# First up stage of the convolution FFN: P1 + P6 summed in PSUM, and the order of four products, for twenty of the 22 features

## The chip, the core and the metric

The kernel runs on one core of a Trainium2 chip. The metric is the device time of one execution in microseconds (us), median of three runs. The engines are named as in the profile: PE (TensorE) multiplies, DVE (VectorE) and ACT (ScalarE) do elementwise work, POOL (GpSimd) does small copies and issues some DMAs, SP (SyncE) issues the other DMAs.

## What is computed

One layer of an encoder for 2048 prompt rows and 128 sample rows of width 1024: attention, an mLSTM, and a convolution FFN. The part that matters here is the first half of the FFN:

```python
def conv_ffn(h, buf, w_up, w_conv, b_conv, w_down):
    u = h @ w_up                       # 1024 -> 2 * 2816
    ext = concatenate([buf, u], axis=1)
    y = b_conv
    for j in range(3):
        y = y + ext[:, j:j + S] * w_conv[j]
    gate, up = split(y, 2, axis=-1)
    return (gelu(gate) * up) @ w_down, ext[:, S:]
```

## The kernel before

The FFN runs in three blocks of rows (`FBLOCKS`), b = 0, 1, 2. Each block has an up stage and a down stage. The up stage goes over 22 features f (128 columns of the gate and the 128 columns of the up half that belong to them) in the order `ORDERS[b]`: 0, 11, 1, 12, 2, 13 and so on. The stage of b = 0 is the first up stage; the change lies in it alone.

For each feature the stage computes a two by two block product by a scheme of seven products instead of eight (Winograd's form of Strassen's). The 768 rows of the block are two halves of 384; seven sums of the activations stand ready in SBUF as tiles `B`. A product is twelve matmuls of 128x384: four pieces of the inner dimension, and for each piece three matmuls (`mm3`), since each fp32 factor is split into a high part (`wuh`, made by a cast on ACT) and a low part (`wul`, made by a subtraction on DVE); the function `split` issues both. So a feature is 7 x 12 = 84 matmuls. The results lie in PSUM: `a` (tile `ua`), `d_` (tile `ub`), and `e` and `c` (the two halves of tile `uec`). Each of these tiles has two buffers, so that feature number n writes into what feature number n-2 of the order has left.

The four weight sums s1 to s4 of a feature (tiles `ws`, line 1344) are formed on DVE in the first block only; POOL writes them to DRAM (`wsd`) for the later blocks. Group g = 0 of a feature's weights is the four factors of P1, P6, P7, P5, group g = 1 the three of P2, P4, P3. Two of three groups go through tiles `wuh`/`wul` with two buffers, the third through four smaller tiles `wu3`. A cast into such a buffer waits until the matmuls of the group that lay there have read it. The raw weights and sums are quarters of 256 KB in eleven buffers (`quad`); SP loads the next ones as these come free.

The combinations of a feature, as the lines stand before: ACT copies `a` to `x1` (line 1638), DVE adds `d_` to give `x2` (line 1640), DVE adds `e` to give `x3` (line 1642), DVE adds `c` for one half of the up result (`second`, line 1501, tile `uu`); ACT copies `a` after P2 was added to it (line 1661, tile `ug`); DVE adds `x2` and `e` after P4 (line 1663), and `x2` and `c` after P3 (line 1501, tile `ug`). The last of these is what frees `uec` for the next feature but one. In the trace x1, x2, x3 are all called `x` (in the order of instructions x0, x1, x2). Then come the convolution (`conv`: ACT line 1520, DVE lines 1521 and 1522, GELU on ACT line 1524), the product of gate and up (line 1673), and the sums of activations for the down stage (`store_a`).

The order of the instructions on each engine is not the order of the code: a scheduler places them by a simulated time line, so a change in one place reorders its neighbourhood on all engines. Each engine then works its own list strictly in order.

Of the kernel before, what the change touches and what calls it, by code (L numbers as in the profile page):

```python
# [13 lines left out]
ALU = mybir.AluOpType  # L14
# [27 lines left out]
FOLD_RATE = 1.0  # L42
FAST = (0, 1, 2)
ORDERS = [[f for k in range(NK) for f in (k, k + NK)] if b in FAST else list(range(NF)) for b in range(3)]
B11, B12, B22, B21 = range(4)
T1, T3, T2, T4 = range(4, 8)
PAIRS += [[(((12, 0), (15, 0)), 0, P, "12"), (((13, 0), (SAMPLE, 0)), P, P, "13"), (((14, 0), (14, 64)), 2 * P, 64, "14")]]
# [3 lines left out]
def hymba_step(ctx: ExitStack, tc: tile.TileContext, I: dict, O: dict):  # L51
    nc = tc.nc
# [50 lines left out]
    def mm3(out, ah, al, bh, bl, start, stop, onto=False):  # L103

        nc.tensor.matmul(out, ah, bh, start=start, stop=False, skip_group_check=onto)  # L105
        nc.tensor.matmul(out, ah, bl, start=False, stop=False, skip_group_check=onto)  # L106
        nc.tensor.matmul(out, al, bh, start=False, stop=stop, skip_group_check=onto)  # L107
# [944 lines left out]
    P1, P6, P7, P5, P2, P4, P3 = range(7)  # L1052
# [13 lines left out]
    def quad(name):  # L1066
        return ffn.p3.tile([P, 512], F32, tag="q", name=name, bufs=11)
# [195 lines left out]
    for n_, (half, gi) in enumerate(seq):  # L1263
# [5 lines left out]
        g = GROUPS[gi]  # L1269
        i = int(g[2])  # L1270
# [61 lines left out]
    def load_quads(b, f, g):  # L1332

        src = lambda i: I["w_up"][f][:, i * 512:(i + 1) * 512]
        if b == 0 and g == 0:
            q = []
            for i in range(4):
                q.append(quad(f"wu{f}_{i}"))
                nc.sync.dma_start(q[i], src(i))
            a11, a12, a22, a21 = q  # L1340
            s1, s2, s3, s4 = [quad(f"ws{f}_{i}") for i in range(4)]
            for o, x, y, op in ((s1, a21, a22, ALU.add), (s2, s1, a11, ALU.subtract), (s3, a11, a21, ALU.subtract),
                                (s4, a12, s2, ALU.subtract)):
                nc.vector.tensor_tensor(o, x, y, op=op)
            for i, o in enumerate((s2, s3, s1, s4)):
                nc.gpsimd.dma_start(wsd[f][:, i * 512:(i + 1) * 512], o)
            raws[f] = [a12, a22, s4]
            return [a11, s2, s3, s1]
        if b == 0:
            return raws.pop(f)  # L1350
        kept = lambda i: wsd[f][:, i * 512:(i + 1) * 512]
        out = []
        for i, s_ in enumerate([[src(0), kept(0), kept(1), kept(2)], [src(1), src(2), kept(3)]][g]):
            r = quad(f"wu{b}_{f}_{g}_{i}")
            nc.sync.dma_start(r, s_)
            out.append(r)
        return out

    def load_up(b, i, g, quads=None):
        f = ORDERS[b][i]  # L1360
        n = 2 * i + g
        nm = f"{b}_{f}_{g}"
        if n % 3 < 2:
            h = wpool.tile([P, 2112], F32R, tag="wh", name=f"wuh{nm}", bufs=2)
            l = wpool.tile([P, 2112], F32R, tag="wl", name=f"wul{nm}", bufs=2)
            at = [(h[:, i * 512:(i + 1) * 512], l[:, i * 512:(i + 1) * 512]) for i in range(4)]
        else:
            t = [p4.tile([P, 1056], F32R, tag="w3", name=f"wu3{nm}_{i}", bufs=4) for i in range(4)]
            at = [tuple(t[2 * x + i // 2][:, i % 2 * 512:i % 2 * 512 + 512] for x in range(2)) for i in range(4)]
        for (h, l), r in zip(at, quads or load_quads(b, f, g)):  # L1370
            split(h, l, r)
        return at
# [111 lines left out]
    for b, tiles in enumerate(FBLOCKS):  # L1484
# [3 lines left out]
        n = HALF[b]  # L1488
# [4 lines left out]
        def product(i, w, acc, onto=False):  # L1493
            for k in range(4):
                c = slice(k * P, (k + 1) * P)
                mm3(acc[:, :n], w[0][:, c], w[1][:, c], B[i][:, 0, k, :n], B[i][:, 1, k, :n],
                    start=not onto and k == 0, stop=k == 3, onto=onto)
# [29 lines left out]
        def ahead_of(i):  # L1527
            if i < 2 * NF:
                pend.append(load_up(b, i // 2, i % 2))
            elif i == 2 * NF:  # L1530
                pend.append(load_product(b, 0, 0) if fast else load_down(0, 0))

        g, parts = {}, {}
        n2 = nt * P // 2

        def fetch(dh, k, early=False):
            if dh > 1 or k >= NF:
                return
            if early:
                g[dh, k] = [quad(f"gr{b}_{dh}_{k}_{i}")[:, :n2] for i in range(2)]  # L1540
                for i, r in enumerate(g[dh, k]):
                    nc.sync.dma_start(r, gd[b][k][:, i * n2:(i + 1) * n2])
            else:
                g[dh, k] = row(f"gr{b}_{dh}_{k}")
                nc.sync.dma_start(g[dh, k][:, :2 * n2], gd[b][k][:, :2 * n2])
# [17 lines left out]
        def fetch_a(i):  # L1563
            if i >= 6 * len(SEQUENCE):
                return
            p, c = divmod(i, 6)
            src = ad[b, SEQUENCE[p][0]]
            ks = slice(2 * c, min(2 * c + 2, NK))
            n_ = (ks.stop - ks.start) * wide(p)
            if i < 5:  # L1570
                g[i] = [quad(f"ar{b}_{i}_{x}")[:, :384] for x in range(2)]
                for x, r in enumerate(g[i]):
                    nc.sync.dma_start(r, src[:, 2 * c + x, :])
            else:
                g[i] = row(f"ar{b}_{i}")[:, :n_]
                nc.sync.dma_start(g[i], src[:, ks, :].rearrange("p k n -> p (k n)"))
# [44 lines left out]
        unfinished = []  # L1621
        for fi, f in enumerate(ORDERS[b]):
            w = pend.pop(0)
            ahead_of(2 * fi + 2)
            if fi >= 3:
                next(done, None)
            if fi == NF - 2:
                for i in range(2):
                    if fast:
                        fetch_a(i)  # L1630
                    else:
                        fetch(0, i, True)
            nm = f"{b}_{f}"
            a, d_, ec = ps_mm(f"ua{nm}"), ps_sm(f"ub{nm}"), ps_big(f"uec{nm}")
            e, c = ec[:, 0:512], ec[:, 512:1024]
            x1, x2, x3 = [p4.tile([P, 384], F32, tag="x", name=f"x{i}_{nm}", bufs=3) for i in range(3)]
            product(P1, w[0], a)
            nc.scalar.copy(x1[:, :n], a[:, :n])
            product(P6, w[1], d_)
            nc.vector.tensor_tensor(x2[:, :n], x1[:, :n], d_[:, :n], op=ALU.add)  # L1640
            product(P7, w[2], e)
            nc.vector.tensor_tensor(x3[:, :n], x2[:, :n], e[:, :n], op=ALU.add)
            product(P5, w[3], c)
            uu = u_tile(f"uu{nm}")
            second(uu, x3, c)
            w = pend.pop(0)
            ahead_of(2 * fi + 3)
            if fi == NF - 1:
                if fast:
                    split_a(0)  # L1650
                    split_a(1)
                    for i in range(2, 5):
                        fetch_a(i)
                else:
                    split_g(0, 0, w3_tile)
                    split_g(0, 1, w3_tile)
                    for k in range(2, 5):
                        fetch(0, k, True)
            ug = u_tile(f"ug{nm}")
            product(P2, w[0], a, onto=True)  # L1660
            nc.scalar.copy(ug[:, 2:2 + n], a[:, :n])
            product(P4, w[1], e, onto=True)
            nc.vector.tensor_tensor(uu[:, 2:2 + n], x2[:, :n], e[:, :n], op=ALU.add)
            product(P3, w[2], c, onto=True)
            second(ug, x2, c)
            yu = conv(uu, 1, f)
            yg = conv(ug, 0, f)
            gt = yg if fast and not last else row(f"g{nm}")
            gv, ov = (lambda t: t[:, :npr]), gt[:, :npr]
            if last:  # L1670
                gv = lambda t: t[:, :npr].rearrange("p (a n) -> p a n", a=2)
                ov = gt[:, :768].rearrange("p (a n) -> p a n", a=2)[:, :, 0:256]
            nc.vector.tensor_tensor(ov, gv(yg), gv(yu), op=ALU.mult)
            if last:
                sv = lambda t: t[:, npr + 2:npr + 2 + DB * (DS + 2)].rearrange("p (b s) -> p b s", b=DB)[:, :, 0:DS]
                nc.vector.tensor_tensor(gt[:, 256:384].rearrange("p (b s) -> p b s", b=DB),
                                        sv(yg), sv(yu), op=ALU.mult)
            if fast:
                store_a(f, gt)
            else:  # L1680
                nc.gpsimd.dma_start(gd[b][f][:, :nt * P], gt[:, :nt * P])
# [5 lines left out]
        if fast:  # L1687
# [73 lines left out]
            kept = {}  # L1761
# [22 lines left out]
            for p, (_, _, set_, onto) in enumerate(SEQUENCE):  # L1784
                for c in range(3):
# [19 lines left out]
                    for k in range(4 * c, min(4 * c + 4, NK)):  # L1805
                        i = 6 * p + k // 2
# [193 lines left out]
```

## Time and profile before

| | |
|---|---|
| median of 3 runs | 2754.65 us (2751.52 to 2759.46) |
| profiled execution | 2753.91 us, its span 2752.2 us |
| PE busy | 97% of the span |
| DVE, ACT, POOL busy | 70%, 53%, 27% |
| first up stage | from 1321 us to about 1648 us of the span |
| of this, 1343 to 1648 us (305 us) | PE busy 301.73, DVE 288.73, ACT 153.86, POOL 167.30 us |

How to read it: the span is the time between the first and the last instruction of the profiled execution. A matmul is shown with its own duration, which overlaps that of the next one; what counts on a full PE is the distance from one start to the next. A bracket behind a row of the time line gives how long the engine stood idle before the instruction, and which engine and line released it.

### The profile page before, as it was taken

How to read it: one execution, taken by the hardware profiler on the slowest of the kernel's cores; microseconds unless marked ns; L12 is line 12 of the kernel's file. 1: busy time of each engine (PE TensorE's matmuls, PEld its weight loads, DVE VectorE, ACT ScalarE, POOL GpSimd, SP SyncE). 2: the span in 40 equal slices, each digit the busy share in tenths (PEclk: the TensorE clock that was granted, in tenths of full speed). 3: DMA queues.
4: the chain of work that ended last, by engine and by line, in shares of the span. 5: the costliest groups of instructions: out<-in, count | busy, mean ns of one | idle time of the engine just before them, and what ended most of it. 6: DMA issues, size and time to landing. Idle time of an engine off the chain costs nothing.

```text
span 2752.2 us, 47852 instructions
## 1 busy us (share of the span) xinstructions
PE 2677.0 (97%) x16323; PEld 2504.0 (91%) x16323; DVE 1922.8 (70%) x3643; ACT 1457.1 (53%) x2961; POOL 731.5 (27%) x1397
## 2 busy tenths in 40 slices
PE   8999999999999999999999999999999999999998
PEld 7899999998899998878999997799999878999976
DVE  5344456646556667766999997758888866998956
ACT  4355545634356666543555456655455665554554
POOL 1000010211100002344465551123343212556401
PEclk9999999999999999999999999999999999999999
DMA  5534355557564456678776668757886867798875
GB/s 185 159 115 141 104 162 169 165 149 213 155 192 131 139 171 223 195 235 279 286 210 197 198 199 286 239 185 209 240 238 184 263 227 233 228 263 233 252 265 178
DMA packets 337172, 557.04 MB, mean 202 GB/s; under 512 B 62083, under 2 KB 168415, under 8 KB 336799
## 3 DMA queue, kind: packets, MB, share of 16 engines
q1 hardware_dynamic: 252846, 400.31, 47.2%
q0 software_dynamic: 45488, 119.84, 14.8%
q10 hardware_dynamic: 38592, 33.83, 3.7%
q8 instruction: 128, 2.10, 0.3%
q14 instruction: 118, 0.96, 0.1%
HBM read 389.77 MB, written 173.49 MB: 205 GB/s over the span
## 4 chain that ended last, share of the span: by engine, by line
PE 43%; DVE 4%; DMA 3%; issue 1%; ACT 1%; POOL 0%; SPq 0%; DVEq 0%; POOLq 0%; ACTq 0%
PE uec L105 5%; PE uec L106 5%; PE uec L107 5%; PE dn L107 3%; PE dn L105 3%; PE dn L106 3%; PE ua L107 3%; PE ua L106 3%; PE ua L105 3%; PE dnm L107 1%; PE dnm L106 1%; PE ub L107 1%; PE dnm L105 1%; PE ub L105 1%; PE ub L106 1%
## 5 line engine op out<-in xcount | busy, mean ns | idle before, releaser
L105 PE MATMUL uec<-B,wuh 128*128 128x384 f32 (+1 forms) x720 | 236.2, 328 | 6.0 <-DVE ug L1501 3.3
L106 PE MATMUL uec<-B,wuh 128*128 128x384 f32 (+1 forms) x720 | 235.3, 327 | 0.0
L107 PE MATMUL uec<-B,wul 128*128 128x384 f32 (+1 forms) x720 | 234.4, 327 | 0.0
L1327 ACT CAST wuh<-wu 128x512 fp32r<-128x512 f32 x255 | 141.7, 618 | 105.9 <-PE uec L106 104.5
L107 PE MATMUL dn<-wdh,al 128*128 128x512 f32 x462 | 186.0, 403 | 4.7 <-DVE al L1328 4.5
L1328 DVE TENSOR_TENSOR al<-ar,ah 128x768 fp32r<-128x768 f32 (+2 forms) x141 | 108.6, 779 | 116.4 <-ACT ah L1327 114.1
L105 PE MATMUL dn<-wdh,ah 128*128 128x512 f32 x462 | 183.8, 398 | 5.9 <-ACT ah L1327 3.7
L106 PE MATMUL dn<-wdl,ah 128*128 128x512 f32 x462 | 182.6, 395 | 0.0
L1327 ACT CAST ah<-ar 128x768 fp32r<-128x768 f32 (+2 forms) x141 | 96.2, 692 | 152.3 <-PE dnm L106 112.9
L1328 DVE TENSOR_TENSOR wul<-wu,wuh 128x512 fp32r<-128x512 f32 x255 | 164.5, 685 | 2.4 <-ACT wuh L1327 2.4
L406 DVE CUSTOM_DVE_ANT_0 tmp<-s,nb 128x640 f32<-128x640 f32 (+4 forms) x128 | 94.4, 738 | 89.9 <-PE s L396 89.3
L105 PE MATMUL vo<-wi_h,hT 128*128 128x256 f32 x544 | 155.2, 285 | 0.6 <-DVE mt L212 0.6
L107 PE MATMUL vo<-wi_h,hT 128*128 128x256 f32 x544 | 155.6, 286 | 0.0
L106 PE MATMUL vo<-wi_l,hT 128*128 128x256 f32 x544 | 154.8, 285 | 0.0
L1328 DVE TENSOR_TENSOR wdl<-wdr,wdh 128x512 fp32r<-128x512 f32 x231 | 145.5, 686 | 8.5 <-ACT wdh L1327 8.3
L105 PEld LDWEIGHTS uec<-B,wuh 128*128 128x128 f32 x720 | 135.2, 188 | 9.2 <-issue 3.7
L106 PEld LDWEIGHTS uec<-B,wuh 128*128 128x128 f32 x720 | 135.4, 188 | 0.2
L107 PEld LDWEIGHTS uec<-B,wul 128*128 128x128 f32 x720 | 135.1, 188 | 0.0
L105 PE MATMUL qk<-hT,wi_h 128*128 128x384 f32 (+1 forms) x384 | 129.0, 336 | 5.9 <-ACT qk_st L237 5.2
L419 DVE TENSOR_TENSOR ptl<-pt,pth 128x640 fp32r<-128x640 f32 (+4 forms) x128 | 93.6, 738 | 57.8 <-ACT pth L418 56.9
L1327 ACT CAST wdh<-wdr 128x512 fp32r<-128x512 f32 x231 | 127.5, 620 | 11.3 <-PE uec L106 7.5
L407 ACT ACTIVATE tmp<-tmp,mn 128x640 f32<-128x640 f32 (+4 forms) x128 | 97.6, 763 | 64.2 <-DVE mn L406 61.8
(426 smaller groups left out, 9258.8 us busy)
## 6 DMA issues: line engine op xcount, KB each, us to landing
wu<-in_w_up SPq DMA_DIRECT2D x220, 256.0 KB, 4.8
wu<-wsd SPq DMA_DIRECT2D x176, 256.0 KB, 3.4
wdr<-wtd SPq DMA_DIRECT2D x132, 256.0 KB, 4.8
wi_raw<-in_w_in SPq DMA_DIRECT2D x52, 512.0 KB, 4.0
wdr<-in_w_down SPq DMA_DIRECT2D x99, 256.0 KB, 4.7
wsd<-ws POOLq DMA_DIRECT2D x88, 256.0 KB, 4.3
ar<-ad_S SPq DMA_DIRECT2D x50, 384.0 KB, 3.4
kraw<-kTd SPq DMA_DIRECT2D x112, 128.0 KB, 3.3
```

The source lines that it names most:

```text
L105: nc.tensor.matmul(out, ah, bh, start=start, stop=False, skip_group_check=onto)
L106: nc.tensor.matmul(out, ah, bl, start=False, stop=False, skip_group_check=onto)
L107: nc.tensor.matmul(out, al, bh, start=False, stop=stop, skip_group_check=onto)
L406: nc.vector.tensor_tensor_reduce(o_, s_, b_, 1.0, 3e38, ALU.add, ALU.min, accum_out=mn)
L407: nc.scalar.activation(tmp[:, :n], tmp[:, :n], AF.Exp, bias=mn, scale=-1.0, accum_out=rsum[:, i % 4, hh:hh + 1])
L419: nc.vector.tensor_tensor(s.ptl[:, sl, qc], ptv, s.pth[:, sl, qc], op=ALU.subtract)
L1327: nc.scalar.copy(h, r)
L1328: nc.vector.tensor_tensor(l, r, h, op=ALU.subtract)
```

## The change

For 20 of the 22 features of the first up stage (the list `SEEDED`: block 0, from the third feature of the order on) `x1 + d_` is no longer an addition on DVE. ACT copies `a`, which holds P1, into the PSUM tile `d_`. P7 is computed next, and then P6 is accumulated by the matmuls onto `d_`. ACT then copies `d_` out to `x2`. The order of the products becomes P1, P7, P6, P5, and the two factors and their sums change places in the lists of weights accordingly; the rest of the feature stays.

```diff
+SEEDED = [(b, f) for b in (0,) for f in ORDERS[b][2:]]
...
-            return [a11, s2, s3, s1]
+            return [a11, s3, s2, s1] if (b, f) in SEEDED else [a11, s2, s3, s1]
...
+        early = (kept(1), kept(0)) if (b, f) in SEEDED else (kept(0), kept(1))
-        for i, s_ in enumerate([[src(0), kept(0), kept(1), kept(2)], [src(1), src(2), kept(3)]][g]):
+        for i, s_ in enumerate([[src(0), *early, kept(2)], [src(1), src(2), kept(3)]][g]):
...
+            seeded = (b, f) in SEEDED
             product(P1, w[0], a)
-            nc.scalar.copy(x1[:, :n], a[:, :n])
-            product(P6, w[1], d_)
-            nc.vector.tensor_tensor(x2[:, :n], x1[:, :n], d_[:, :n], op=ALU.add)
-            product(P7, w[2], e)
+            if seeded:
+                nc.scalar.copy(d_[:, :n], a[:, :n])
+                product(P7, w[1], e)
+                product(P6, w[2], d_, onto=True)
+                nc.scalar.copy(x2[:, :n], d_[:, :n])
+            else:
+                nc.scalar.copy(x1[:, :n], a[:, :n])
+                product(P6, w[1], d_)
+                nc.vector.tensor_tensor(x2[:, :n], x1[:, :n], d_[:, :n], op=ALU.add)
+                product(P7, w[2], e)
             nc.vector.tensor_tensor(x3[:, :n], x2[:, :n], e[:, :n], op=ALU.add)
             product(P5, w[3], c)
```

On each engine the instructions outside the first up stage and the start of the down stage behind it stand in the same order as before. Inside the stage the order is new. Counted in matmuls from the first one of the stage (1848 in all), the products stand as follows at three neighbouring features (first matmul to the one behind the last; a product can be interleaved with others):

| product | f15 before | f15 after | f5 before | f5 after | f16 before | f16 after |
|---|---|---|---|---|---|---|
| P1 | 732-758 | 732-756 | 780-816 | 768-816 | 900-916 | 912-926 |
| P6 | 734-768 | 770-782 | 816-840 | 840-852 | 902-926 | 936-948 |
| P7 | 768-780 | 756-768 | 840-852 | 828-840 | 904-936 | 914-936 |
| P5 | 824-836 | 816-828 | 888-900 | 876-888 | 960-972 | 972-984 |
| P2 | 781-805 | 782-806 | 852-876 | 852-876 | 936-960 | 948-972 |
| P4 | 854-866 | 854-866 | 940-952 | 900-912 | 988-1000 | 1008-1020 |
| P3 | 876-888 | 888-900 | 972-984 | 951-963 | 1043-1055 | 1046-1058 |

The pattern repeats: before, every third feature (252 matmuls) P7 begins 16 matmuls after the last P3 matmul of the feature whose `uec` buffer it takes. The six such places are P7 of f13, f4, f16, f7, f19 and f10. After, the distance at these six is 14, 17, 14, 14, 17 and 14.

VectorE's list around the place where the buffer of `uec` is freed for feature 16. In the names the first number behind the letters is the block, the second the feature, the last a running number; `ws0`, `ws1` of a feature are two of its weight sums (here `ws6_0` is the first sum of feature 6, made of two freshly loaded quarters), `ug0_15` is the addition that frees the buffer. First the list before:

```order
L1663 TENSOR_TENSOR uu0_15_17885<-x1_0_15_17832,uec0_15_17830 128x384
L1673 TENSOR_TENSOR y0_4_0_17788<-y0_4_0_17788,y0_4_1_17782 128x768
L1642 TENSOR_TENSOR x2_0_5_17995<-x1_0_5_17994,uec0_5_17992 128x384
L1344 TENSOR_TENSOR ws6_0_18125<-wu6_3_18123,wu6_2_18121 128x512
L1615 TENSOR_TENSOR s3_0_4_17953<-y0_4_0_17788 128x384
L1521 SCALAR_TENSOR_TENSOR y0_15_1_17937<-uu0_15_17885,wcv_16366,y0_15_1_17937 128x768
L1344 TENSOR_TENSOR ws6_1_18126<-ws6_0_18125,wu6_0_18117 128x512
L1501 TENSOR_TENSOR ug0_15_17895<-x1_0_15_17832,uec0_15_17830 128x384
```

The same stretch after (line numbers of the changed code: 1345 is the old 1344, 1503 the old 1501, 1524 the old 1522, 1672 the old 1663):

```order
L1672 TENSOR_TENSOR uu0_15_17885<-x1_0_15_17832,uec0_15_17830 128x384
L1682 TENSOR_TENSOR y0_4_0_17788<-y0_4_0_17788,y0_4_1_17782 128x768
L1345 TENSOR_TENSOR ws6_0_18125<-wu6_3_18123,wu6_2_18121 128x512
L1617 TENSOR_TENSOR s3_0_4_17953<-y0_4_0_17788 128x384
L1523 SCALAR_TENSOR_TENSOR y0_15_1_17937<-uu0_15_17885,wcv_16366,y0_15_1_17937 128x768
L1345 TENSOR_TENSOR ws6_1_18126<-ws6_0_18125,wu6_0_18117 128x512
L1503 TENSOR_TENSOR uu0_5_18047<-x2_0_5_17995,uec0_5_17992 128x384
L1329 TENSOR_TENSOR wu30_16_1_3_18052<-ws16_3_17973,wu30_16_1_1_18050 128x512
L1524 SCALAR_TENSOR_TENSOR y0_15_1_17937<-uu0_15_17885,wcv_16366,y0_15_1_17937 128x768
L1503 TENSOR_TENSOR ug0_15_17895<-x1_0_15_17832,uec0_15_17830 128x384
```

Between the first weight sum and the addition that frees the buffer stand three more instructions now, and the addition `x2_0_5` stands ahead of this stretch.

PE's list at the first two matmuls of P2 of feature 3, which use the first quarter of group 1 of its weights (`wuh0_3_1`). Before:

```order
L106 MATMUL uec0_3_17358<-B2_0_15356,wuh0_3_0_17162 128x384
L107 MATMUL uec0_3_17358<-B2_0_15356,wul0_3_0_17163 128x384
L105 MATMUL ua0_14_17509<-B0_0_15354,wu30_14_0_0_17324 128x384
L105 MATMUL ua0_3_17356<-B4_0_16344,wuh0_3_1_17251 128x384
L106 MATMUL ua0_3_17356<-B4_0_16344,wuh0_3_1_17251 128x384
```

After (106, 107, 108 are the old 105, 106, 107):

```order
L106 MATMUL uec0_13_17194<-B3_0_16340,wuh0_13_0_17007 128x384
L107 MATMUL uec0_13_17194<-B3_0_16340,wuh0_13_0_17007 128x384
L108 MATMUL uec0_13_17194<-B3_0_16340,wul0_13_0_17008 128x384
L106 MATMUL ua0_3_17356<-B4_0_16344,wuh0_3_1_17251 128x384
L107 MATMUL ua0_3_17356<-B4_0_16344,wuh0_3_1_17251 128x384
L106 MATMUL uec0_13_17194<-B5_0_16348,wu30_13_1_0_17096 128x384
```

P2 of feature 3 now begins directly behind the last matmuls of P5 of feature 13, that is, behind the last readers of `wuh0_13_0`. The same stands at feature 18 behind feature 7.

ACT's list around the copy of P1 at feature 16. Before:

```order
L1520 ACTIVATE y0_15_0_17943<-ug0_15_17895,wcv_16366 128x768
L1661 COPY ug0_5_18059<-ua0_5_17990 128x384
L1638 COPY x0_0_16_18148<-ua0_16_18145 128x384
L1524 ACTIVATE y0_15_0_17943<-y0_15_0_17943 128x768
L1520 ACTIVATE y0_5_1_18101<-uu0_5_18047,wcv_16366 128x768
```

After (1642 is the copy onto `d_`, 1645 the copy out of it, 1522 the old 1520, 1526 the old 1524):

```order
L1670 COPY ug0_5_18059<-ua0_5_17990 128x384
L1522 ACTIVATE y0_15_0_17943<-ug0_15_17895,wcv_16366 128x768
L1642 COPY ub0_16_18146<-ua0_16_18145 128x384
L1522 ACTIVATE y0_5_1_18101<-uu0_5_18047,wcv_16366 128x768
L1645 COPY x1_0_16_18149<-ub0_16_18146 128x384
L1526 ACTIVATE y0_15_0_17943<-y0_15_0_17943 128x768
```

The copy onto `d_` follows an instruction that reads what DVE's `ug0_15` wrote, and a second copy has come in ahead of the GELU.

## The prediction

> **What bounds the kernel now.** I read the page first, then the busy time in the stretch that the change touches.
>
> ```profile
> span 2752.2 us, 47852 instructions
> PE 2677.0 (97%) x16323; PEld 2504.0 (91%) x16323; DVE 1922.8 (70%) x3643; ACT 1457.1 (53%) x2961; POOL 731.5 (27%) x1397
> ...
> 1343.00:1648.00 305.00, 301.73 (x1714) 298.93 (x1713) 288.73 (x451) 153.86 (x245) 167.30 (x252) 0.99 0.66 201
> ```
>
> The second row is the page's busy time by engine, the last one the stretch of the 20 changed features (length, then busy us of PE, weight loads, DVE, ACT, POOL). PE is full there, and DVE is the next: 288.73 of 305 us, 95%. ACT has half its time free. So the change takes work from the second engine, not from the first, and can win only what PE loses by waiting. What that is, the time line of PE tells. The rows show start, duration, and in the bracket the idle time before it with its releaser.
>
> ```profile
> 1394.00 0.44 PE L107 MATMUL ua<-B,wul 128*128 128x384 f32 x1
> ...
> 1481.72 0.33 PE L106 MATMUL ub<-B,wuh 128*128 128x384 f32 x1
> 1483.52 0.41 PE L105 MATMUL uec<-B,wuh 128*128 128x384 f32 x1 [1.47 <-DVE ug L1501]
> ...
> 1484.31 0.34 PE L105 MATMUL ua<-B,wuh 128*128 128x384 f32 x1
> ...
> 1527.49 0.33 PE L106 MATMUL ub<-B,wuh 128*128 128x384 f32 x1
> ...
> 1571.98 0.33 PE L106 MATMUL ub<-B,wuh 128*128 128x384 f32 x1
> 1573.94 0.41 PE L105 MATMUL uec<-B,wuh 128*128 128x384 f32 x1 [1.62 <-DVE ug L1501]
> ...
> 1574.95 0.52 PE L106 MATMUL ua<-B,wuh 128*128 128x384 f32 x1
> ...
> 1578.15 0.38 PE L106 MATMUL ub<-B,wuh 128*128 128x384 f32 x1
> ...
> 1620.03 0.45 PE L107 MATMUL ua<-B,wul 128*128 128x384 f32 x1
> ```
>
> From 1484.31 to 1527.49 lie 248 matmuls: 0.1741 us each is PE's undisturbed step. The rows at 1394.00 and 1620.03 are the same place of the pattern (the first low-part matmul of P1 of f13 and of f10), five periods of 252 matmuls apart: 226.03 us, against 1260 x 0.1741 = 219.4. So PE loses 6.7 us over 15 of the 20 features. It loses it at one kind of place, P7 waiting for the addition `ug` that frees its `uec` buffer: at f16 (1481.72 to 1484.31, four steps) 2.59 - 0.70 = 1.89 us, at f19 (1571.98 to 1574.95, five steps) 2.97 - 0.87 = 2.10, and then at half speed (1574.95 to 1578.15, ten steps in 3.20 us) 1.46. The other three places share 1.2. Part of each is a slow restart: from 1483.52 to 1484.31 three steps take 0.79 us, 0.27 too much. Why DVE is late there, its own time line shows:
>
> ```profile
> 1434.44 0.69 DVE L1344 TENSOR_TENSOR ws<-wu,wu 128x512 f32<-128x512 f32 x1 [1.26 <-DMA wu<-in_w_up]
> ...
> 1480.21 0.69 DVE L1344 TENSOR_TENSOR ws<-wu,wu 128x512 f32<-128x512 f32 x1 [2.79 <-DMA wu<-in_w_up]
> 1480.82 0.55 DVE L1615 TENSOR_TENSOR s<-y 128x384 f32<-128x384 f32 x1
> 1481.29 1.01 DVE L1521 SCALAR_TENSOR_TENSOR y<-uu,wcv,y 128x768 f32<-128x768 f32 x1
> 1482.22 0.68 DVE L1344 TENSOR_TENSOR ws<-ws,wu 128x512 f32<-128x512 f32 x1
> 1482.82 0.55 DVE L1501 TENSOR_TENSOR ug<-x,uec 128x384 f32<-128x384 f32 x1
> ...
> 1524.69 0.69 DVE L1344 TENSOR_TENSOR ws<-wu,wu 128x512 f32<-128x512 f32 x1 [1.50 <-DMA wu<-in_w_up]
> ...
> 1570.64 0.69 DVE L1344 TENSOR_TENSOR ws<-wu,wu 128x512 f32<-128x512 f32 x1 [2.95 <-DMA wu<-in_w_up]
> ```
>
> Once in a period the first weight sum of a feature waits for the loads of its raw weights, and everything behind it in DVE's list is late. Waits of 2.79 and 2.95 us cost PE the two big stops; waits of 1.26 and 1.50 us nearly nothing. About 1.3 us is slack. And the load, by the chain of waits, starts when a split of weights on DVE has freed a raw buffer:
>
> ```profile
> 1562.60 0.70 DVE wul L1328
> 1563.32 7.23 DMA wu<-in_w_up
> ```
>
> **The change part by part.** *The addition removed, the copy added.*
>
> ```profile
> L1640 DVE TENSOR_TENSOR x<-x,ub 128x384 f32<-128x384 f32 x19 | 10.4, 549 | 0.0
> ...
> 1412.04 0.34 PE L107 MATMUL ua<-B,wul 128*128 128x384 f32 x1
> ...
> 1412.41 0.48 ACT L1638 COPY x<-ua 128x384 f32<-128x384 f32 x1 [1.20 <-PE ua L107]
> ```
>
> DVE loses 20 x 0.549 = 11.0 us, and is then busy 277.7 of 305 (91%). ACT gains 20 x 0.48 = 9.6 us on 153.9. Neither is on the path by itself: the sum of both is nothing, as long as ACT's copy is there in time.
>
> *The new wait of P6 for the copy onto `d_`.* The rows at 1412 give it: the copy starts 0.37 us after the last P1 matmul started and takes 0.48. From the end of an addition on DVE to the matmul that waited for it (1482.82 + 0.55 to 1483.52) 0.15 us pass; I take the same from ACT. So P6 may start 1.00 us after P1's last matmul started. By the order 10 matmuls stand between at f3, f4, f16, f18, f19 and f10, at the others 12 to 24: at least 11 x 0.1741 = 1.91 us. P7 hides the copy with 0.91 us to spare, and the cost is 0. No row here shows a copy written to PSUM; the rows bound it by 0.48 into SBUF below and by the 0.91 of spare above (a copy would have to take three times as long to be seen). The Trainium skill (ScalarE: Activation LUTs, "Step-by-step: what each stage is for") says that PSUM is the faster target for ScalarE; that would only add to the spare, and no run here shows it.
>
> *The places where DVE frees `uec`.* At f16, as the lists show, PE now gives 48 matmuls from P4 of f15 to P7 instead of 38: 10 x 0.1741 = 1.74 us more for DVE. DVE has three more instructions between the weight sum and `ug`: by the steps in the rows above (0.47 for 384 elements, 0.60 for 512, 0.93 for the convolution) 2.00 us more. The load comes earlier: the split that frees its buffer waits for P5 of f15, which ends at matmul 828 instead of 836, 1.39 us, less one weight sum that has moved ahead of the split, 0.60. Sum: 1.74 - 2.00 + 0.79 = 0.53 us in favour of the change. I take it for all the places: f16 and f19 gain 0.53 each, the three small ones (0.4 each) vanish, 1.2. The half speed came behind a gap of 1.96 us and not behind one of 1.80 (1481.72 to 1483.52); with the gap at f19 at 1.43 I take it as gone, 1.46. Together -3.7 us. Bounds: 0, if the loads land as late as before, and -6.7, if all goes.
>
> The Trainium skill (TensorE: Matmul & The Clock Gate, "Part 1: The HAM clock gate") has PE fall to half clock after an idle window of about 3.4 us. The trace disagrees with the length of the idle time, 1.96 us here, and the measurement decides; by the page the half speed would not hang on this stop, and the sum would be 1.5 us higher.
>
> *New waits for casts.* P2 of f3, and of f18, now stands directly behind P5 of the feature whose weight buffer it takes.
>
> ```profile
> 1405.24 0.34 PE L106 MATMUL uec<-B,wuh 128*128 128x384 f32 x1
> ...
> 1405.65 0.62 ACT L1327 CAST wuh<-wu 128x512 fp32r<-128x512 f32 x1 [1.74 <-PE uec L106]
> ```
>
> These rows show the same hand-over before: the cast starts 0.41 us after the last reader of the buffer started, takes 0.62, and with 0.15 the first matmul can start 1.18 us behind that reader. The new order gives it two steps, 0.35: a stop of 0.83 and a restart of 0.27, 1.1 us, twice. P1 of f4, and of f19, stands five steps behind the last such reader (0.87): 0.31 + 0.27, 0.6 us, twice. Together +3.4 us. Bounds: 0, if that buffer is freed by another group, and 5.2, if each of the four costs a full 1.3 (no step of cover).
>
> **The sum**, against the profiled execution's 2753.9: -3.7 + 3.4 = -0.3, so 2753.6. The median before is 0.7 above that execution, well within the runs' range; as a median I forecast 2754.3: no change. All shares below count by 0.3%, 8.3 us, about what a measurement of this kernel can tell from no change.
>
> **The rivals.**
>
> *A, the stage runs without a gap.* If DVE's 11 us of relief bring the loads so early that no place stops and the casts are hidden, the whole 6.7 us go: 2747.2, as a median 2748. For it speaks that DVE's share falls from 95 to 91%; against it that three instructions have moved ahead of `ug`. To pass 8.3 us the waits at the start of the down stage must go too, 2.1 us by the rows of PE's waits:
>
> ```profile
> PE dn L105 <- ACT wdh L1327: 1.7, 2, 1.2
> PE dn L105 <- ACT ah L1327: 0.4, 1, 0.4
> ```
>
> that is 2745.1. Chance of A 0.19, of it 0.06 beyond 0.3%.
>
> *B, slower: the copy onto `d_` stands in ACT's queue behind an instruction that waits for DVE, and PE waits with it.* ACT does wait like that:
>
> ```profile
> L1524 ACT ACTIVATE y<-y 128x768 f32<-128x768 f32 x19 | 16.1, 847 | 51.9 <-DVE y L1522 51.9
> ```
>
> 2.7 us each time. If a wait like it stands ahead of the copy at the six places with 1.91 us of cover, each stops PE for 2.7 - 0.91 + 0.27 = 2.1 us: 12.4 in all, 2766.0, as a median 2767. If half speed follows every stop, 1.46 each time, it is 2775. It decides from about 2 us of lateness at all six (1.4 us each make 8.3). Against it: in ACT's new list none of the six copies comes directly behind line 1524; at f16 it follows the convolution's first step, whose input `ug` is due 22 matmuls, 3.8 us, before P6. For it: `ug` has moved back on DVE, and the queue gives nothing back. Chance 0.20.
>
> *C, the loads set the pace, and DVE's relief changes nothing.* The stops stay as they are and the four new waits come on top: 2753.9 + 3.4 = 2757.3, as a median 2758. For it: the wait that counts is one for DMA, of 7.23 us in the row above. Against it: its start hangs on a split that the new order frees earlier. Chance 0.16.
>
> **How the numbers follow.** My forecast has 0.45, and with C and most of A everything within 0.3% has 0.45 + 0.16 + 0.13 = 0.74; faster 0.06; slower 0.20. The range goes from A, 2748, to the lighter form of B, 2767; outside are the rest of A and the heavy form of B, some 0.15.
>
> **What would show it.** Right: in the stretch DVE is busy about 11 us less and ACT 10 us more; PE waits less for `ug` at line 1503, about 2 us for casts at two places before P2 of `ua` and two before P1, and not at all for ACT's copy before `ub`. Wrong: waits of `ub` for line 1642 (B), or the same brackets of 1.5 us behind `ug` (C), or a distance from the first place to the last of 219.4 us (A).

## The result and the profile after

The changed kernel takes 2765.32 us (median of 6 runs, 2760.73 to 2769.30) against 2754.58 (6 runs) for the kernel before. The ratio on record is 1.0032, 95% interval 1.0019 to 1.0046 (the quotient of the two medians is 1.0039). Two repetitions gave 1.0050 (1.0033 to 1.0066) and 1.0027 (1.0013 to 1.0041). So it is slower by about 0.3 to 0.5%, 7 to 14 us. The forecast was no change.

The page of the changed kernel, and the same 305 us of the stage as before (they begin 22 us behind the first matmul of the stage in both):

```profile
span 2766.0 us, 47853 instructions
PE 2682.6 (97%) x16323; PEld 2509.7 (91%) x16323; DVE 1914.6 (69%) x3623; ACT 1465.0 (53%) x2981; POOL 723.5 (26%) x1397
1352.45:1657.45 305.00, 297.25 (x1682) 293.54 (x1682) 276.55 (x424) 160.28 (x262) 164.19 (x249) 0.99 0.66 199
```

DVE is busy 12.2 us less (288.73 to 276.55) and ACT 6.4 us more (153.86 to 160.28). The forecast had 11 and 10 for the whole set of features, and the 305 us now hold a little less of the stage. But PE, the engine that is full, is busy 4.5 us less in the same time and has done 32 matmuls less. The waits of PE in the stage say for what (who waited, for which engine and line; us in total, times, longest). First before, then after:

```profile
PE uec L105 <- DVE ug L1501: 3.3, 3, 1.6
PE ua L107 <- DVE wul L1328: 1.2, 2, 0.7
PE uec L105 <- DVE x L1642: 0.7, 1, 0.7
PE dn L105 <- ACT wdh L1327: 0.5, 1, 0.5
```

```profile
PE uec L106 <- DVE x L1651: 4.3, 3, 1.8
PE uec L106 <- ACT wuh L1328: 2.2, 1, 2.2
PE ua L108 <- DVE wul L1329: 1.3, 2, 0.9
PE ua L106 <- ACT wuh L1328: 1.1, 2, 0.5
PE uec L106 <- DVE uu L1503: 0.7, 2, 0.5
```

The row for `ug` is gone: in this profile P7 no longer waits for it. Instead PE waits 4.3 us for `x` (x3), where it was 0.7 before, and at one place 2.2 us before P4. The first of the three waits for `x` (0.7) lies at the stage's start, as before. The other two are P5 of f14 and of f8. ACT, DVE and PE at f14, from the time line:

```profile
1443.90 0.46 ACT L1645 COPY x<-ub 128x384 f32<-128x384 f32 x1
...
1445.94 0.69 DVE L1345 TENSOR_TENSOR ws<-wu,wu 128x512 f32<-128x512 f32 x1 [1.62 <-DMA wu<-in_w_up]
...
1448.35 0.69 DVE L1345 TENSOR_TENSOR ws<-ws,wu 128x512 f32<-128x512 f32 x1
1448.95 0.55 DVE L1651 TENSOR_TENSOR x<-x,uec 128x384 f32<-128x384 f32 x1
...
1447.45 0.33 PE L107 MATMUL ua<-B,wuh 128*128 128x384 f32 x1
1449.55 0.45 PE L106 MATMUL uec<-B,wu 128*128 128x384 f32 x1 [1.77 <-DVE x L1651]
```

x2 is there at 1444.36. The addition x3, which needs only x2 and P7, starts 4.6 us later, because in DVE's list it stands behind two weight sums of f15, and the first of them waits 1.62 us for its load. In the code P5 writes the half `c` of `uec`, while x3 reads the half `e`; the row shows that P5 waited for it all the same, so the wait is taken for the whole tile. Before, x3 stood one row ahead of those sums at this place:

```profile
1432.63 0.55 DVE L1642 TENSOR_TENSOR x<-x,uec 128x384 f32<-128x384 f32 x1
1434.44 0.69 DVE L1344 TENSOR_TENSOR ws<-wu,wu 128x512 f32<-128x512 f32 x1 [1.26 <-DMA wu<-in_w_up]
```

The new order also left P5 less room: between P6 and P5 of f14, and of f8, lie 26 matmuls, 4.5 us, where before it was 48, 8.4 us. P4 of f5 is the same, with `uu` in place of x3, behind the sums of f6:

```profile
1494.34 0.69 DVE L1345 TENSOR_TENSOR ws<-wu,wu 128x512 f32<-128x512 f32 x1 [3.33 <-DMA wu<-in_w_up]
...
1496.94 0.55 DVE L1503 TENSOR_TENSOR uu<-x,uec 128x384 f32<-128x384 f32 x1
...
1497.64 0.41 PE L106 MATMUL uec<-B,wuh 128*128 128x384 f32 x1 [2.17 <-ACT wuh L1328]
```

The bracket names ACT, one of whose casts ended at the same time as `uu`, 1497.49. It is `uu` that counts: in the second profile of the changed kernel that cast ended only after the same matmul had started, and the row names `uu`:

```profile
1488.70 0.41 PE L106 MATMUL uec<-B,wuh 128*128 128x384 f32 x1 [1.85 <-DVE uu L1503]
```

In DVE's list of waits, the weight sums before and after (same 305 us):

```profile
DVE ws L1344 <- DMA wu<-in_w_up: 10.7, 6, 2.9
...
DVE ws L1345 <- DMA wu<-in_w_up: 14.9, 11, 3.3
```

DVE, with less to do, waits for its loads more often: of the 12.2 us by which it is less busy, 4.2 are these waits (they are 9.6 and 17.6 us in the next profiles of the two kernels).

**Where the time lies.** Every profile has the same 16323 matmul records, so two matmuls mark the same points in all kernels: the first of the stage, and one of the second up stage, 2597 records later. Of before, then after:

```profile
1320.96 0.34 PE L105 MATMUL ub<-B,wuh 128*128 128x384 f32 x1
...
1826.09 0.34 PE L107 MATMUL ua<-B,wul 128*128 128x384 f32 x1
```

```profile
1330.41 0.34 PE L106 MATMUL ub<-B,wuh 128*128 128x384 f32 x1
...
1838.35 0.34 PE L108 MATMUL ua<-B,wul 128*128 128x384 f32 x1
```

505.1 us and 507.9. So of the 13.4 us between the two profiled executions only 2.8 lie in the stage and the down stage behind it (5.6 lost up to the down stage's first matmul, 2.8 given back in the down stage); 9 lie ahead of the stage, where both kernels have the same instructions in the same order. The table holds these stretches for all profiles (us, between the starts of matmuls in the traces; the first column begins at the program's first matmul, the third ends at its last), with the ratio to the kernel before, which was measured anew for each group of runs.

| kernel | to the stage | the stage and its down stage | the rest | ratio (95%) |
|---|---|---|---|---|
| before | 1312.7 | 505.1 | 917.0 | |
| before, again | 1313.9 | 502.4 | 916.4 | 1.0005 (0.9994-1.0015) |
| changed | 1321.8 | 507.9 | 918.6 | 1.0032 (1.0019-1.0046) |
| changed, 2nd | 1314.9 | 508.0 | 918.2 | 1.0050 (1.0033-1.0066) |
| changed, 3rd | 1312.0 | 510.6 | 918.8 | 1.0027 (1.0013-1.0041) |
| order alone | 1318.9 | 499.6 | 914.6 | 0.9997 (0.9987-1.0008) |
| seeding alone | 1312.0 | 505.1 | 920.4 | 1.0007 (0.9997-1.0017) |
| P6 last | 1315.2 | 502.9 | 917.6 | 1.0015 (1.0006-1.0024) |
| addition put back | 1309.7 | 512.4 | 915.5 | 1.0011 (1.0000-1.0022) |
| sums behind x3 | 1321.7 | 503.3 | 917.2 | 0.9992 (0.9981-1.0003) |
| sums behind uu | 1316.6 | 503.0 | 919.1 | 1.0011 (1.0000-1.0022) |
| two places pinned | 1319.8 | 505.1 | 917.6 | 1.0004 (0.9991-1.0017) |
| before, sums behind ug | 1312.0 | 497.5 | 915.6 | 0.9972 (0.9960-0.9985) |
| changed, sums behind ug | 1312.3 | 494.6 | 917.8 | 0.9976 (0.9962-0.9989) |

### The profile page after: what moved, and what is told of

Its sections match the earlier page's. It is cut to its first block, busy times and chain, and to the rows that moved or that the text cites. A ratio compares the mean times of both kernels' runs of the same rounds, so it can differ in the third digit from the quotient of the medians.

```text
span 2766.0 us, 47853 instructions
## 1 busy us (share of the span) xinstructions
PE 2682.6 (97%) x16323; PEld 2509.7 (91%) x16323; DVE 1914.6 (69%) x3623; ACT 1465.0 (53%) x2981; POOL 723.5 (26%) x1397
## 3 DMA queue, kind: packets, MB, share of 16 engines
q0 software_dynamic: 45488, 119.84, 14.9%
## 4 chain that ended last, share of the span: by engine, by line
PE 42%; DMA 4%; DVE 4%; issue 1%; ACT 1%; POOL 0%; DVEq 0%; POOLq 0%; SPq 0%; ACTq 0%
PE uec L106 5%; PE uec L107 5%; PE uec L108 5%; PE dn L108 4%; PE dn L106 3%; PE dn L107 3%; PE ua L108 3%; PE ua L107 2%; PE ua L106 2%; PE dnm L108 1%; PE dnm L107 1%; PE dnm L106 1%; DMA wu<-in_w_up 1%; PE ub L107 1%; PE ub L106 1%
```

## The experiments

**Controls.** Both kernels unchanged, to see which part of the 13.4 us belongs to the change.

> The kernel before, unchanged, as a control. Both theories: ratio 1.000 within 0.1%. The two profiled executions so far differ by 13.4 us at the end, of which 9.2 us were there before the first up stage, where both kernels give the same instructions in the same order. If those 9.2 us are an accident of the execution (T1), this profile's distance from the start to the first matmul of the stage may lie anywhere within some 10 us of the earlier one; if they belong to the changed kernel (T2), it agrees with the first profile of before within 3 us.

> The changed kernel, unchanged, as a control. T1 (the change costs what its own stage shows, about 5 us, and the rest is an accident): ratio 1.001 to 1.0025 and, in its profile, the way up to the stage is no longer than in the control of before by more than 4 us. T2 (something of the change costs outside its stage too): ratio 1.003 to 1.005, and the 9 us ahead of the stage are there again. Both: inside the stage PE stops about 2 us for P5 at f14 and f8 behind x3 on DVE, and about 2.4 us for P4 at f5 behind uu.

The ratio was that of T2 (1.0050), the place was that of T1: the changed kernel came to the stage 1.1 us behind the control of before. The stage with its down stage was 5.6 us longer (508.0 and 502.4), with the same stops and one more behind `uu`, 1.7 us, later in the stage:

```profile
PE uec L106 <- DVE uu L1503: 3.8, 3, 1.8
PE uec L106 <- DVE x L1651: 3.6, 3, 1.6
```

> The changed kernel, unchanged, on the chip of the run with two places pinned, with a third profile. Two questions. The ratio: 1.003 to 1.005 as before. The way up to the stage, where both kernels give the same instructions: 9.2 and 2.1 us longer than in the first profile of before in the two profiles so far. If that is an accident of the half-speed stretches (about 1.7 us each, 1 to 6 of them ahead of the stage in the ten profiles), it goes with their number here too, within 3 us; if it belongs to the changed kernel, it is 4 us or more whatever their number.

The third profile reached the stage 0.7 us earlier than the first of before. The 9 us were an accident of one execution; T2 falls as far as the way up is concerned. The stops were there again (`uu` 4.5 us in all, 2.84 of it at f5; `x` 3.7).

**The two halves of the change apart.** First the new order of products and weights without the seeding:

```diff
             product(P1, w[0], a)
             if seeded:
-                nc.scalar.copy(d_[:, :n], a[:, :n])
+                nc.scalar.copy(x1[:, :n], a[:, :n])
                 product(P7, w[1], e)
-                product(P6, w[2], d_, onto=True)
-                nc.scalar.copy(x2[:, :n], d_[:, :n])
+                product(P6, w[2], d_)
+                nc.vector.tensor_tensor(x2[:, :n], x1[:, :n], d_[:, :n], op=ALU.add)
```

> Products and weights in the new order P1 P7 P6 P5, but P1 is still copied to x1 in SBUF and added to P6 on DVE (no copy onto PSUM, 20 additions of 0.549 us back on DVE, ACT as after). Theory S (the stops come from the order, which puts P5 behind x3, with P6 so late): the stage is as long as in the changed kernel or longer, ratio 1.002 to 1.007, since DVE has 11 us more to do ahead of x3; stops of about 2 us at P5 again. Rival K (the copy onto PSUM on ACT and the matmul that adds onto it are what costs): the stage is as long as before, ratio 0.999 to 1.001.

I had expected the order to be what hurts. Alone it does not: 0.9997, and the stretch is shorter than before (499.6). But this kernel does not set P5 as near behind P6 as the changed kernel does: 48 matmuls lie between them at f14 and 36 at f8, not 26. And x3 of f14 stands ahead of the sums again. No stop of P5 is left but the early one:

```profile
PE ua L106 <- ACT wuh L1328: 1.6, 3, 0.5
PE ua L108 <- DVE wul L1329: 1.0, 2, 0.6
PE uec L106 <- DVE x L1651: 0.7, 1, 0.7
...
DVE ws L1345 <- DMA wu<-in_w_up: 3.1, 3, 1.4
```

With 11 us more to do, DVE waits for loads 3.1 us instead of 14.9. That gave the theory R: the weight sums, and where the scheduler sets them in DVE's list once it has time to spare. The other half, seeding with the old order P1 P6 P7 P5:

```diff
-            return [a11, s3, s2, s1] if (b, f) in SEEDED else [a11, s2, s3, s1]
+            return [a11, s2, s3, s1]
...
-                product(P7, w[1], e)
-                product(P6, w[2], d_, onto=True)
+                product(P6, w[1], d_, onto=True)
                 nc.scalar.copy(x2[:, :n], d_[:, :n])
+                product(P7, w[2], e)
```

> Seeded as in the changed kernel (copy of P1 onto the PSUM tile by ACT, P6 summed onto it, copy out by ACT), but products and weights in the old order P1 P6 P7 P5: the fourth corner beside before, the changed kernel and the one with the new order alone. Theory R (taking the addition off DVE lets the scheduler set the weight sums, which wait for DMA, ahead of the additions x3 and uu that P5 and P4 wait for; the order of the products is innocent): stops at P5 and P4 as in the changed kernel, DVE waits for DMA 10 times or more, ratio 1.002 to 1.005. Rival O (it takes the new order and the seeding together): 0.999 to 1.001.

1.0007: the number is that of O. Half of R held: DVE waits for loads 10 times again.

```profile
DVE ws L1345 <- DMA wu<-in_w_up: 12.4, 10, 2.0
```

But at f14 and f8 x3 stands in its list directly behind the first sum, not four rows behind it, and P5 does not stop there; the two largest stops that are left, 1.4 and 1.5 us start to start, are P7 of f4 and f19. So waiting for loads is not the loss by itself; what counts is what stands behind the wait. Here 34 matmuls lie between P6 and P5 at f14 and f8. Only both halves together set x3 four rows behind the sum and P5 26 matmuls behind P6; this run does not say which of the two makes the stop.

**P6 moved behind P5**, so that P5 no longer comes after x3:

```diff
-            return [a11, s3, s2, s1] if (b, f) in SEEDED else [a11, s2, s3, s1]
+            return [a11, s3, s1, s2] if (b, f) in SEEDED else [a11, s2, s3, s1]
...
                 product(P7, w[1], e)
-                product(P6, w[2], d_, onto=True)
+                product(P5, w[2], c)
+                product(P6, w[3], d_, onto=True)
...
-            product(P5, w[3], c)
+            if not seeded:
+                product(P5, w[3], c)
```

> Seeded as in the changed kernel, but the products come in the order P1 P7 P5 P6: P5 no longer stands behind x3 in any feature, since it is given ahead of the P6 that x3 waits for, and P4 stands 36 matmuls or more behind P5. Theory S: the stops of 2 us at P5 and P4 go, DVE keeps its 11 us of relief, and the stage is 3 to 6 us shorter than in the changed kernel: ratio 0.998 to 1.001. Stops for casts may remain, 1 to 3 us. Rival K (the seeding costs): as long as the changed kernel, 1.002 to 1.005.

1.0015, between the two ranges: the stops of P5 went and the stretch is 5 to 8 us shorter than in the changed kernel, but other waits took part of it back: P4 behind `uu` once, and more at the start for the low part of a weight. That last wait lies ahead of the change; the other profiles have it too, with 0.4 to 1.2 us.

```profile
1326.57 0.44 PE L108 MATMUL ua<-B,wul 128*128 128x384 f32 x1 [1.82 <-DVE wul L1329]
...
1562.50 0.44 PE L106 MATMUL uec<-B,wuh 128*128 128x384 f32 x1 [1.54 <-DVE uu L1503]
```

**The addition put back** as work that nothing uses:

```diff
                 nc.scalar.copy(x2[:, :n], d_[:, :n])
+                nc.vector.tensor_tensor(x1[:, :n], x2[:, :n], d_[:, :n], op=ALU.add)
```

> The changed kernel with 20 additions put back on DVE that nothing uses (x2 + d_ into a tile of x's pool), each where the removed one stood. Everything that the change adds on ACT and PE stays. Theory R: with DVE's time filled again, the weight sums go back behind x3 (no place with two sums ahead of x3, as there are at f14 and f8 in the changed kernel), the two stops of 2.1 us at P5 go, and the kernel gets faster by doing more: 0.999 to 1.0015. Rival A (the copies on ACT, 10 us more and in the chain from P6 to x3, are what costs): no gain, 1.003 to 1.006, or more since DVE has 11 us more to do.

1.0011 is R's number, but it settles little: its interval overlaps that of the changed kernel's third measurement on the same chip, and its profile has the longest stretch of all (512.4). P5 of f14 and f8 do not stop (36 matmuls lie between P6 and P5 there), but a product at the stage's end waits 1.7 us for x3, and the old stops behind `ug` are back, one of them doubled:

```profile
1572.96 0.41 PE L106 MATMUL uec<-B,wuh 128*128 128x384 f32 x1 [3.09 <-DVE ug L1503]
```

**The sums pinned.** In the next kernels nothing is computed otherwise than in the changed kernel; the four sums of a feature are only queued on DVE behind a mark of the feature two places earlier:

```diff
+            i = ORDERS[b].index(f)
+            with tc.issue_after(marks[i - 2]) if i - 2 in marks else nullcontext():
-            for o, x, y, op in (...):
-                nc.vector.tensor_tensor(o, x, y, op=op)
+                for o, x, y, op in (...):
+                    nc.vector.tensor_tensor(o, x, y, op=op)
...
-            nc.vector.tensor_tensor(x3[:, :n], x2[:, :n], e[:, :n], op=ALU.add)
+            x3_ = nc.vector.tensor_tensor(x3[:, :n], x2[:, :n], e[:, :n], op=ALU.add)
+            if seeded:
+                marks[fi] = x3_.ins
```

> The changed kernel, in which the four weight sums of a feature are queued on DVE behind the addition x3 of the feature two places earlier in the order. Theory R: x3 never stands behind a wait for DMA, so the stops at P5 of f14 and f8 (2.15 and 2.10 us, and the half speed behind one of them) go; the one at P4 of f5 (2.5 us) stays, since uu still stands behind a sum there: 2 to 5 us less than the changed kernel, ratio 1.001 to 1.003. Rival A: the stops at P5 stay, since x3 waits for ACT: 1.003 to 1.006.

0.9992, better than R asked: the loss is gone. The stops of P5 went, and P4 of f5 lost 1.01 us (start to start) instead of 2.51. DVE still waits for loads, and the loss is gone all the same:

```profile
DVE ws L1347 <- DMA wu<-in_w_up: 12.3, 10, 2.6
...
PE uec L106 <- DVE uu L1505: 1.4, 3, 0.7
PE ua L108 <- DVE wul L1329: 1.2, 2, 0.8
PE uec L106 <- DVE ug L1505: 0.8, 2, 0.6
```

With the mark at `uu` instead (the addition of `c`):

> The changed kernel, in which the four weight sums of a feature are queued on DVE behind the addition uu (P5's result) of the feature two places earlier in the order, so that neither x3 nor uu stands behind them. Theory R: the stops at P5 and P4 all go, 5 to 7 us less than the changed kernel, ratio 0.999 to 1.002; what could eat that: the sums come later, so casts or low parts of the weights are late (waits of PE for wul or wuh), up to 3 us. Rival A: 1.003 to 1.006.

1.0011, inside R's range. The stops at P5 and P4 are gone and DVE waits for loads only 3.0 us, but the sums come later and PE waits 3.3 us for low parts of weights (four times), as was feared.

Then the mark `if seeded and f in (14, 8)`, so that only the sums of f15 and f9 are pinned:

> The changed kernel, in which only at two places, f14 and f8, the weight sums are queued on DVE behind x3 (sums of f15 and f9); the rest of the order is nearly that of the changed kernel. These are the two places where two sums stood ahead of x3 and PE stopped 2.1 us for P5. Theory R: both stops go, 4 to 6 us with the half speed behind one of them: ratio 1.000 to 1.003, and 4 us or more below the changed kernel on the same chip. Rival D (the loss is spread over many small waits, and the pins of all features together brought it back): at most 1 us less than the changed kernel, 1.003 to 1.005.

1.0004 against 1.0027 for the changed kernel on the same chip: medians of 2753.87 and 2760.32 us, 6.5 us from pins at two places, and rival D falls. At f14 the two rows of DVE have changed places, and P5 has no bracket, although only 24 matmuls lie between P6 and P5 there, two fewer than in the changed kernel. So it is the place of x3 behind the waiting sums that made the stop, not the distance by itself:

```profile
1443.29 0.54 DVE L1653 TENSOR_TENSOR x<-x,uec 128x384 f32<-128x384 f32 x1
1443.75 0.68 DVE L1347 TENSOR_TENSOR ws<-wu,wu 128x512 f32<-128x512 f32 x1
```

Not all of the 6.5 us was lost at the two places themselves. P5 lost 3.3 us there in the third profile of the changed kernel; P4 of f5, whose sums are not pinned, also lost less, 1.31 us from start to start instead of 3.18, and no half speed followed as it did there. Why f5 lost less is not shown.

**The same in the kernel before.** There it was `ug` that stood behind the sums of the feature three places later:

```diff
+            with tc.issue_after(marks[i - 3]) if i - 3 in marks else nullcontext():
...
-            second(ug, x2, c)
+            ug_ = second(ug, x2, c)
+            if b == 0 and fi >= 2:
+                marks[fi] = ug_.ins
```

> The kernel before, in which the weight sums of a feature are queued on DVE behind the addition ug of the feature three places earlier, which frees the PSUM buffer that P7 waits for. No seeding, old order of products. Theory R (what PE loses in this stage is decided by the sums that wait for DMA ahead of what PE waits for): the stops of 1.5 us behind ug go, 2 to 5 us less than before, ratio 0.998 to 0.9995. Rival L (the loads set the pace, and what is gained at ug is lost as late casts or low parts of weights): 0.9995 to 1.001.

0.9972, 2745.19 us: 8 us less than before, and more than theory R asked for. From the stage's first matmul to the one ahead of the down stage's first there are 1823 steps; at 0.1741 us each they take 317.4 us. The kernel before took 9.8 us more (7.1 in its second profile), the changed kernel 15.4 (14.3 and 16.9 in the others), this one 4.3. All that is left of PE's waits in the stage, and no weight sum among DVE's waits any more:

```profile
PE ua L107 <- DVE wul L1328: 1.4, 2, 1.0
PE uec L105 <- DVE x L1643: 0.8, 1, 0.8
PE uec L105 <- DVE uu L1664: 0.5, 2, 0.3
PE dn L105 <- ACT wdh L1327: 0.5, 1, 0.5
```

And the changed kernel with the same pin (`if seeded:` in place of `if b == 0 and fi >= 2:`):

> The changed kernel with the pin that made the kernel before faster: the weight sums of a feature are queued on DVE behind the addition ug of the feature three places earlier. By the order no x3 stands behind a sum then; uu still does at eight features, five to seven rows on. Theory R: the changed kernel loses its stops at P5, the sums come late enough that they seldom wait for DMA (under 5 us in all instead of 15 to 18): ratio 0.997 to 0.9995, and what is left of the change itself, once the order on DVE is mended in both, is 0 to 4 us of loss from casts (four places at 0.5 us) and from P4 behind uu. Rival W (the relief of DVE is worth something once the sums are out of the way): faster than the pinned kernel before, below 0.996.

0.9976, 2743.77 us, and in the trace the shortest stretch of all, 494.6 us (3.8 us above the undisturbed pace in the stage):

```profile
PE ua L108 <- DVE wul L1329: 1.2, 2, 0.7
PE uec L106 <- DVE x L1652: 0.7, 1, 0.7
PE uec L106 <- DVE uu L1505: 0.3, 1, 0.3
```

No wait for a load, and none for a cast at the four places. It is not faster than the pinned kernel before by anything that the intervals show; W falls. With the sums out of the way, no gain and no cost of the change itself can be told from nothing: the medians of the two pinned kernels are 1.4 us apart, and each ratio is known to about 0.13%, 3.6 us.

## Why the prediction was wrong

*What bounds the kernel: right.* PE is full, and what DVE is late with is decided by weight sums that wait for loads. The last two experiments show it: with these sums behind `ug`, 5.5 of the 9.8 us are gone in the stage (2.8 of the 7.1 in the control), and most of what is left lies at its start, ahead of the change.

*"It loses it at one kind of place": the step that failed.* I worked out the new distances for P7 and `ug` alone. But x3 and `uu` read the same tile `uec`, and P5 and P4 write it. Rows of before showed such a wait (P5 of the first feature, 0.7 us for `x` at line 1642), and the order showed that x3 moves from one row ahead of the sums to four rows behind the first of them at f14 and f8. I followed that shift for `ug` only. The order showed besides that P5 comes nearer to P6, from 48 matmuls to 26 at these two features, and I used the new positions for the copy, the casts and P7, not for x3. Its cost: 2.10 and 2.15 us from start to start at P5, 2.51 at P4 of f5, 0.79 and 0.61 at P4 of two more; less a step of 0.174 each that is 7.3, with 1.5 of half speed behind f8 8.8 us. The sum contained 0 for all of it. The kernel pinned at two places shows the cause at P5: with x3 ahead of the sums the two stops are gone, and the kernel is 6.5 us faster, a part of it at f5.

*The places where DVE frees `uec`: right in sign, too small.* -3.7 was forecast; all stops behind `ug` went (1.62, 1.78 and 0.33 us by the same count), and the half speed that followed one of them: -5.2, with the slow restarts nearer to the bound of -6.7. In the other two profiles of the changed kernel a wait of 0.1 and of 0.4 us for `ug` is left. So the advance was larger than the assumed 0.53 us. The stops of PE at P5 and P4 lie ahead of P7 and may have given DVE the time there; no run separates that.

*Casts: right in place, too dear.* 3.4 us forecast, 1.8 measured:

```profile
1424.95 0.34 PE L108 MATMUL uec<-B,wul 128*128 128x384 f32 x1
1425.82 0.45 PE L106 MATMUL ua<-B,wuh 128*128 128x384 f32 x1 [0.53 <-ACT wuh L1328]
...
1446.81 0.34 PE L108 MATMUL ua<-B,wul 128*128 128x384 f32 x1
1447.17 0.44 PE L106 MATMUL ua<-B,wuh 128*128 128x384 f32 x1
```

P2 of f3 loses 0.70 us (1.1 forecast), P1 of f4 0.19 (0.6), and the same at f18 and f19; these losses are counted without the restart, which takes 0.1 us more each time where I had set 0.27. With -5.2, +8.8 and +1.8 the stage comes to +5.4; this pair of traces has +5.6. Other pairs have other sizes: from 9.8 or 7.1 before to 14.3, 15.4 or 16.9 after it is 4.5 to 9.8 us.

*P6's wait for the copy: right.* No row has `ub` waiting for line 1642. The two copies:

```profile
L1645 ACT COPY x<-ub 128x384 f32<-128x384 f32 x20 | 9.5, 475 | 22.1 <-PE ub L108 22.1
L1642 ACT COPY ub<-ua 128x384 f32<-128x384 f32 x20 | 9.3, 463 | 18.2 <-PE ua L108 18.1
```

The Trainium skill's statement that PSUM is ScalarE's faster target (ScalarE: Activation LUTs, "Step-by-step: what each stage is for") agrees in sign: 463 against 475 ns.

*The rivals.* B had nearly the right number, 2767, by a mechanism that did not occur; that was luck. C was right that relief of DVE does not bring loads earlier (waits for them grew from 10.7 to 14.9 us), but wrong that the old stops stay. What came was a third: with time to spare on DVE the scheduler set the sums ahead of what PE waits for next, while P5 moved nearer to P6.

*What stays open.* The ratios put the loss at 7 to 14 us, the medians at 7 to 11. The three traces show 4.5 to 9.8 in the stage, of which 3 to 8 are left at the end of its down stage, and 1 to 2 behind that, where the spread among all kernels (914.6 to 920.4) is larger than that. The rest I could not place: the way up to the stage varies from 1309.7 to 1321.8 us by itself. Not tried: `e` and `c` as tiles of their own, which might take the wait of P5 for x3 away without a pin.

## What to carry to other kernels

When an engine is relieved and a scheduler orders it, look at what moves up into the room: an instruction that waits for DMA, set ahead of one that the full engine waits for, can cost more than the work that was saved is worth. For a tile whose halves are used by different instructions, list every reader and writer at its new distance, not only the one that waits now. And a wait is worth removing only with a view to what is queued behind it: pinning the sums behind one addition took 8 us from the kernel before and brought the changed one to the same time, while the kernel pinned behind x3 ran at 0.9992 with 12 us of DVE's waits for loads still in it.

## What I had not expected of the hardware

In the traces' records of the granted clock every stretch of half speed starts a whole multiple of 3.413 us from the others of its execution and lasts 3.413 us, or twice that (the last one of each runs past the program's end). In the stage and its down stage, over 14 profiles, half speed came eight times. To see what it followed, count in each 3.413-us cell of this grid by how much the starts of matmuls lie further apart than the undisturbed step (0.174 us for 384 columns, 0.232 for 512). Half speed followed the cells with 2.06 to 3.07 us of such idle time, and no other at full speed; the fullest of the others had 2.03, so the border lies near 60% of a cell. So the same stop costs 1.5 us more or not, as it falls within a cell or across its border: at f14 (2.10 us) nothing followed, at f8 (2.15) it did. The Trainium skill (TensorE: Matmul & The Clock Gate, "Part 1: The HAM clock gate") has the free-running window of 3413 ns, and the traces agree; that a whole idle window is needed they do not bear out, since about 60% of one was enough. Much of the scatter of single executions goes with it: ahead of the stage there were 1 to 6 such stretches (one of double length counted twice), and the way up is longer by 2.1 us for each (a straight line through the 14 profiles, correlation 0.88).
